# A hybrid decoder layer on one core: buffer places, deferred sums and engine choice in its MLP tail

## Chip, core and metric

One core of a Trainium2 chip runs the whole layer. The engines are TensorE (PE, the matrix products), VectorE (DVE), ScalarE (ACT) and GpSimd (POOL); SyncE (SP) issues most transfers, in order, as ACT does a few. The metric is the device time of one execution in microseconds (us), less is better.

## What is computed

The reference is a decoder layer on 1024 tokens of width 1024 in float32: three branches (a matrix-memory recurrence, a differential attention, a cross-attention into 256 memory tokens), gates that weigh them, an output projection, and an MLP. Only its end matters here:

```python
merged = g_m * (y_m @ w_proj_m[l]) + g_d * (y_d @ w_proj_d[l]) + g_c * (y_c @ w_proj_c[l])
x = x + merged @ w_out[l]

h2 = rms_norm(x, norm_mlp_g[l])
x = x + jnp.square(jax.nn.relu(h2 @ w_up[l])) @ w_down[l]
```

`w_up` is 1024 x 4096, `w_down` 4096 x 1024.

## The kernel before

All values are held with features on partitions and tokens along the free axis, as tiles of 128 x 512 (two halves `hf` of the tokens). A float32 product is made of three matmuls on a high and a low part of each operand (`mm3`, L119); an operand is split by a cast on ACT (high part) and a subtraction on DVE (low part), by `split` or, in a stretch whose order is pinned, `split2`. Every matmul is written by the helper at L93. A scheduler reorders instructions of DVE, ACT, POOL and SP by its own estimates, while PE keeps the written order in the pinned stretches; the rows below are the order that comes out.

**Merge and output projection** (`tail`, L1410 on). For each branch the products `mm<-kt,w` are weighed with gate tiles. Then `wout` is multiplied: for each of 8 feature tiles and 2 halves, `res` loads a tile of the input x into a `gl` tile (`fetch`, L1418), adds the product (L1476), stores it (x1_d, L1477), squares it (`sq`, L1482), sums the squares on POOL (`ssq`, L1483), and scales it into `h2` (L1485), which is stored. The pool `gl` has two places, which gates and x tiles take in turn.

**Up projection** (`wino`). Products of 2 x 2 blocks are made by seven products instead of eight (Strassen in Winograd's form): a block step n is seven products of three matmuls each, 21 matmuls of 128 x 512. A unit u is one of 16 column blocks of `w_up` and takes four steps (kp 0 to 3, the four row blocks of `h2`); its seven sums p0 to p6 stand in seven of the eight PSUM banks. `raw` loads a weight block (256 KB, `wraw`) and makes four of its eight forms on POOL (L1260 to L1263), `wsp` splits it into `wo`, up to three steps ahead. `wino_x` makes the operand `xo` from `h2` (`xr`, with sums `xts`). Unit 0 is done in two runs, because the last part of `h2` comes late: steps 0 and 1 on kp 0 and 1, then unit 1 (steps 2 to 5), then steps 6 and 7. Its first run's sums are copied to seven `pt` tiles (two of them in `gl`, two in `ssq`).

The factor of the norm (`rb`) is made on the way: `rstd` is a generator; `first(bank)` moves it on at four places between products: `px<-ones,ssq` (sums over the squares), then the reciprocal root and the diagonal tiles `dg`, then two products `px<-dg,ones`, copied by ACT into the two halves of `rb` (L1544).

After a unit `combine` makes four results from the seven sums (one copy on ACT, seven sums on DVE: tiles `u2`, `c11`, `u3`, `c21`, shown as `u` and `c`). `use_up` multiplies each with `rb` on DVE, takes relu and square on ACT into `rq`, stores three of them, and after a `yield` makes the four operand sums `xts` of the down projection (`wino_t`, three on DVE and one on POOL, L1243) and stores them to r_d. For unit 0 (`whole`) `combine` works in place on the `pt` tiles. `todo` says after which step each piece runs.

**Down projection** (`down`). The same scheme: steps of 21 matmuls `p<-xd,wo`; `xd` is the operand read back from r_d (three sums in place 0 to 2, four in 3 to 6), split in place. Its tiles lie in memory that the up projection's tiles leave, and so wait for their last readers. There are three places for raw weights (dwr0 to dwr2). `x02` holds the last two of the first operand's seven forms. Below, d0, d1, ... are the down projection's raw weights in order, x0, x1, ... its operands.

Of the kernel before, what the change touches and what calls it, by code (L numbers as in the profile page):

```python
# [10 lines left out]
F32 = mybir.dt.float32  # L11
# [6 lines left out]
P = 128  # L18
# [55 lines left out]
class Layer:  # L74
# [1214 lines left out]
    def wino(self, ws, load, use, first, parts):  # L1289


        V, A = self.V, self.A
        self.pinned = True

        runs = [(0, (0, 1)), (1, (0, 1, 2, 3)), (0, (2, 3))] + [(u, (0, 1, 2, 3)) for u in range(2, len(ws))]
        raw, wsp, W = self.wino_steps([ws[u][:, kp] for u, kps in runs for kp in kps], self.wrp, self.wop, 3)
        X = {}
        raw()
        wsp(0, self.split)
        X[0] = self.wino_x(0, load)  # L1300
        wsp(0, self.split)
        X[1] = self.wino_x(1, load)
        X[2] = self.wino_x(2, load)
        raw()
        wsp(0, self.split)
        tl = lambda n: self.ev.tile([P, 512], F32, tag=n, name=self.name(n))

        def combine(ms, psum):

            m1, m2, m6, m7, m4, m5, m3 = ms  # L1310
            u2, c11, u3, c21 = m1, m2, m7, m4
            if psum:
                u2, c11, u3, c21 = (tl(n) for n in ("u2", "c11", "u3", "c21"))
                A.copy(u2, m1)
            V.tensor_add(c11, u2, m2)
            V.tensor_add(u2, u2, m6)
            V.tensor_add(u3, u2, m7)
            V.tensor_add(c21, u3, m4)
            V.tensor_add(u3, u3, m5)
            V.tensor_add(u2, u2, m5)  # L1320
            V.tensor_add(u2, u2, m3)
            return u2, c11, u3, c21


        todo = {}
        n = -1
        for r, (u, kps) in enumerate(runs):
            bank = lambda j: f"p{(7 * r + j + 4) % 8}"
            ps = [self.pw.tile([P, 512], F32, tag=bank(j), name=self.name(f"p{j}")) for j in range(7)]
            for kp in kps:  # L1330
                n += 1
                if n == 2:
                    X[3] = self.wino_x(3, load)
                w, x = W[n], X[kp]
                for j, (l, q) in enumerate(self.PROD):
                    self.mm3(ps[j], (w[:, l, 0], w[:, l, 1]), (x[:, q, 0], x[:, q, 1]), kp == kps[0], kp == kps[-1])
                    if (r, kp, j) in ((0, 1, 1), (1, 1, 6), (1, 2, 6), (1, 3, 3)):
                        first(bank(7))
                if kp != kps[-1]:
                    wsp(n)  # L1340
                    for f in todo.pop(n, []):
                        next(f)
            if r == 0:
                part = parts()
                for t, m in zip(part, ps):
                    A.copy(t, m)
                wsp(n)
            elif r == 2:
                for t, m in zip(part, ps):
                    V.tensor_add(t, t, m)  # L1350
                wsp(n)


                def whole():
                    c = combine(part, False)
                    yield
                    yield from use(0, c)

                next(late)
                g = whole()  # L1360
                todo.update({n + 1: [late], n + 3: [g], n + 5: [g], n + 8: [g]})
            else:
                cs = combine(ps, True)
                wsp(n)
                g = use(u, cs)
                if r == 1:
                    late = g
                else:
                    for f in todo.pop(n, []):
                        next(f)  # L1370
                    next(g)
                    todo.setdefault(n + 1, []).append(g)
        for g in sum(todo.values(), []):
            next(g)
        self.nwino = len(runs)
        self.pinned = False
# [35 lines left out]
    def tail(self):  # L1412
        tc, nc, a = self.tc, self.nc, self.a
        V, G = nc.vector, nc.gpsimd
# [1 line left out]
        cut = lambda t, i, hf: t[:, i, hf * 512 : (hf + 1) * 512]  # L1416

        def fetch(d, f, hf):  # L1418
            t = self.gl.tile([P, 512], F32, tag="gl", name=self.name("gl"))
            nc.sync.dma_start(t, half(d, f, hf))  # L1420
            return t

        c9 = ExitStack()
        with ExitStack() as c0:
            E = lambda *x, **k: c0.enter_context(tc.tile_pool(*x, **k))
# [3 lines left out]
            rb = one.tile([P, D], F32, name="rb2")  # L1429
# [4 lines left out]
            with ExitStack() as c1:  # L1434
                E = lambda *x, **k: c1.enter_context(tc.tile_pool(*x, **k))
                self.pmm, self.kmm, self.nmm = Banks(E, "pmm2"), 8, 3
                if True:
# [7 lines left out]
                    rawp = E(name="yrp", bufs=2)  # L1445
                    self.rp = E(name="rp2", bufs=2)
                    self.wp = E(name="wp2", bufs=4)
                    hi = [[mtp.tile([P, 512], F32R, name=f"mh{k}_{hf}") for hf in range(2)] for k in range(NK)]
                    mg, lo = {}, {}
                    for bi, b in enumerate((2, 0, 1)):  # L1450
# [41 lines left out]
            with ExitStack() as c1:  # L1492
                E = lambda *x, **k: c1.enter_context(tc.tile_pool(*x, **k))
                one_ = lambda n: E(name=n, bufs=1)
# [17 lines left out]
                def use_up(u, cs):  # L1512

                    b = self.xrp.tile([P, 4, 512], F32, tag="xr", name=self.name("rq"))
                    for i in (1, 3, 2, 0):
                        hf = i % 2
                        self.V.tensor_mul(cs[i], cs[i], rb[:, hf * 512 : (hf + 1) * 512])
                        self.A.activation(cs[i], cs[i], AF.Relu)
                        self.A.activation(b[:, i], cs[i], AF.Square)
                    self.A.dma_start(self.rd[u, :, 0:3], b[:, 1:4])  # L1520
                    yield
                    t = self.wino_t(b, self.V)
                    nc.sync.dma_start(self.rd[u, :, 3:7], t)
                    yield

# [34 lines left out]
    def down(self):  # L1560
# [4 lines left out]
        with ExitStack() as c1:  # L1565
# [11 lines left out]
            x3 = one_("dx3")  # L1577
            a1 = one_("acc1")
            accum(a1, 14, 0)
            x02 = one_("dx02")  # L1580
            a2 = one_("acc2")
            accum(a2, 4, 0)
            wr = [one_("dwr2")]
            a3 = one_("acc3")
            accum(a3, 8, 768)
            x1, x2 = one_("dx1"), one_("dx2")
            wr = Ring([one_("dwr0"), one_("dwr1")] + wr)
            wo = Ring([one_(f"dwo{i}") for i in range(3)])
            x00 = one_("dx00")
            accs = accs[2:] + accs[:2]  # L1590
# [16 lines left out]
            def xdma(q):  # L1607

                X[q] = []
                for pool, i, n in xp[q % 4]:  # L1610
                    t = pool.tile([P, n, 2, 512], F32R, tag=f"x{i}", name=self.name("xd"))
                    nc.sync.dma_start(f32(t[:, :, 1]), self.rd[kp(q), :, i : i + n])
                    X[q].append(t)

            def xsplit(q, parts=(0, 1, 2), split=self.split2):
                for i, t in enumerate(X[q]):
                    if i in parts:
                        split(t[:, :, 0], t[:, :, 1], f32(t[:, :, 1]))
# [22 lines left out]
            xsplit(0, split=self.split)  # L1641
            wsp(0, self.split, False)
            xdma(1)
            wsp(0, self.split)
            xsplit(1, split=self.split)
            xdma(2)
            wsp(0, self.split)
            xsplit(2, split=self.split)
            xdma(3)
            n = -1  # L1650
            seen = set()
# [248 lines left out]
```

## Time and profile before

| | us |
|---|---|
| median of 3 runs | 2200.8 (2197.91 to 2201.39) |
| profiled execution, its own time | 2198.07 |
| its span on the core | 2196.3 |
| merge and output projection, end of the last wout product | 1561 |
| up projection | 1561 to 1880 |
| down projection | 1880 to 2192 |

The mean granted clock of PE is 0.996 of full speed. A row of the view of waits says which engine and line waited for which, with the total, the count and the longest. A row of the view of windows has the stretch, its length, the busy time of PE, of its weight loads, of DVE, ACT and POOL, with the number of instructions, then the granted clock, the DMA engines' busy share and GB/s. A row of the timeline has start, duration, engine, line, operation, output and inputs, and in brackets how long the engine stood idle before it and what ended that. Rows on a tile give the fewest, median and most ns and the first and last start.

### The profile page before, as it was taken

The numbers are of one execution on the slowest core, as the hardware profiler recorded it, in microseconds if no ns is written. First come the engines' busy times: TensorE is split into PE (matmuls) and PEld (weight loads), VectorE is DVE, ScalarE is ACT, GpSimd is POOL, SyncE is SP. The second block draws the span as 40 slices with busy tenths as digits, with TensorE's granted clock in tenths as the row PEclk, the third lists the DMA queues.
The fourth block names the chain that finished last, engine by engine and source line by source line (L and its number), as shares of the span: only waits on it lengthen the run. The fifth ranks groups of instructions, "written<-read, shape, count | busy, mean of one in ns | idle before, by whom it ended". The sixth has DMA issues, their size and how long they took to land.

```text
span 2196.3 us, 30710 instructions
## 1 busy us (share of the span) xinstructions
PE 2154.0 (98%) x11049; PEld 1853.4 (84%) x11049; DVE 1424.0 (65%) x2678; ACT 1002.6 (46%) x1998; POOL 571.6 (26%) x732
## 2 busy tenths in 40 slices
PE   7999999999999999999999999999999999999999
PEld 5878889898899999999887788888787888788887
DVE  6643565575548777777665433554589877867779
ACT  6543354454346666666554221223444444643332
POOL 2100000000111111111121002202757655665553
PEclk9999999999999999999999999999999999999999
DMA  6123122121443343333343643435435444954444
GB/s 245 37 72 116 60 89 70 44 82 49 157 119 92 96 97 86 86 87 80 108 158 121 206 144 125 139 115 190 155 116 199 157 144 153 330 192 157 145 140 168
DMA packets 137358, 281.46 MB, mean 128 GB/s; under 512 B 13137, under 2 KB 29814, under 8 KB 135158
## 3 DMA queue, kind: packets, MB, share of 16 engines
q1 hardware_dynamic: 130870, 259.58, 37.5%
q10 hardware_dynamic: 6336, 19.93, 2.3%
q8 instruction: 87, 1.43, 0.3%
q14 instruction: 65, 0.53, 0.1%
HBM read 182.95 MB, written 71.34 MB: 116 GB/s over the span
## 4 chain that ended last, share of the span: by engine, by line
PE 79%; DMA 7%; DVE 6%; ACT 3%; POOL 2%; issue 2%; SPq 0%; DVEq 0%; ACTq 0%; POOLq 0%
PE mm L93 46%; PE p L93 21%; PE sc L93 6%; PE po L93 3%; PE tp L96 3%; DMA x_d<-gl 1%; DVE acc L69 1%; DVE wo L69 1%; DMA gl<-in_xT 1%; PE pr L96 1%; DMA xr<-h_d 1%; DVE u L69 1%; DMA kraw<-y 1%; POOL wraw L1262 0%; DVE w L114 0%
## 5 line engine op out<-in xcount | busy, mean ns | idle before, releaser
L93 PE MATMUL mm<-w,hT 128*128 128x384 f32 (+3 forms) x2496 | 472.9, 332 | 2.9 <-ACT w L113 2.4
L93 PE MATMUL mm<-hT,w 128*128 128x512 f32 x1680 | 411.8, 396 | 0.0
L93 PEld LDWEIGHTS mm<-w,hT 128*128 128x128 f32 x2496 | 390.2, 190 | 14.5 <-ACT w L113 3.0
L93 PEld LDWEIGHTS mm<-hT,w 128*128 128x128 f32 x1680 | 308.5, 188 | 64.7
L93 PE MATMUL p<-xo,wo 128*128 128x512 f32 x1344 | 309.7, 392 | 3.1 <-DVE u L69 1.6
L93 PE MATMUL p<-xd,wo 128*128 128x512 f32 x1344 | 307.8, 391 | 3.8 <-DVE u L69 1.9
L93 PEld LDWEIGHTS p<-xd,wo 128*128 128x128 f32 x1344 | 252.9, 189 | 58.5 <-DVE u L69 2.6
L93 PEld LDWEIGHTS p<-xo,wo 128*128 128x128 f32 x1344 | 252.2, 189 | 59.3 <-DVE u L69 3.7
L93 PE MATMUL mm<-kt,w 128*128 128x512 f32 x1152 | 264.5, 391 | 4.0 <-ACT kt L113 2.7
L93 PEld LDWEIGHTS mm<-kt,w 128*128 128x128 f32 x1152 | 216.8, 189 | 51.7 <-ACT kt L113 3.8
L113 ACT CAST w<-raw 128x256 fp32r<-128x256 f32 (+3 forms) x272 | 142.2, 545 | 164.7 <-PE mm L93 123.2
L114 DVE TENSOR_TENSOR w<-raw,w 128x256 fp32r<-128x256 f32 (+3 forms) x272 | 162.7, 619 | 80.0 <-ACT w L113 78.6
L106 ACT CAST wo<-wraw 128x896 fp32r<-128x896 f32 x122 | 115.0, 944 | 206.6 <-PE p L93 112.0
L69 DVE TENSOR_TENSOR wo<-wraw,wo 128x896 fp32r<-128x896 f32 x122 | 144.3, 1200 | 57.0 <-ACT wo L106 57.0
L1260 POOL TENSOR_TENSOR wraw<-wraw 128x128 f32<-128x128 f32 x128 | 95.1, 743 | 238.4 <-DMA wraw<-in_wdown 103.5
L1008 ACT ACTIVATE dpe<-sc,dst,drr 128x256 f32<-128x256 f32 (+7 forms) x128 | 106.8, 834 | 97.6 <-DVE dst L1004 95.4
L129 POOL TENSOR_SCALAR hss<-hss 128x4 f32<-128x4 f32 x8 | 3.3, 411 | 416.0 <-ACT mscr L754 273.3
L1000 DVE CUSTOM_DVE_ANT_0 sc<-sc,tmask 128x256 f32<-128x256 f32 (+7 forms) x128 | 97.0, 758 | 13.3 <-PE sc L93 12.6
L1263 POOL TENSOR_TENSOR wraw<-wraw 128x128 f32<-128x128 f32 x128 | 93.9, 733 | 10.0
L93 PE MATMUL sc<-dk,dq 128*128 128x512 f32 (+3 forms) x384 | 92.2, 348 | 0.0
L1262 POOL TENSOR_TENSOR wraw<-wraw 128x128 f32<-128x128 f32 x128 | 91.8, 717 | 0.0
L106 ACT CAST xd<-xd 128x1536 fp32r<-128x1536 f32 (+2 forms) x36 | 54.9, 1528 | 67.7 <-DMA xd<-r_d 67.7
(308 smaller groups left out, 3087.6 us busy)
## 6 DMA issues: line engine op xcount, KB each, us to landing
dk<-dsg SPq DMA_DIRECT2D x64, 256.0 KB, 4.5
wraw<-in_wup SPq DMA_DIRECT2D x64, 256.0 KB, 3.3
r_d<-xts SPq DMA_DIRECT2D x16, 1024.0 KB, 4.1
wraw<-in_wdown SPq DMA_DIRECT2D x64, 256.0 KB, 3.0
xd<-r_d SPq DMA_DIRECT2D x19, 768.0 KB, 7.3
xd<-r_d SPq DMA_DIRECT2D x14, 1024.0 KB, 7.0
raw<-in_wd SPq DMA_DIRECT2D x32, 384.0 KB, 3.2
kraw<-y SPq DMA_DIRECT2D x24, 512.0 KB, 4.5
```

The costliest lines, as they stand in the source:

```text
L69: return self.tc.keep_in_program_order(f(*a, **k))
L93: self.pin(self.nc.tensor.matmul(out, l, r, start=start, stop=stop))
L96: self.pin(self.nc.tensor.transpose(out, x, self.ident))
L106: self.A.copy(hi, src)
L113: nc.scalar.copy(hi, src)
L114: nc.vector.tensor_sub(lo, src, f32(hi))
L129: g.tensor_scalar(r, ss, 1.0 / width, EPS, op0=ALU.mult, op1=ALU.add)
L1000: V.tensor_tensor_reduce(out=sc[:, 0:n], in0=sc[:, 0:n], in1=self.tmask[:, D - n : D], scale=1.0, scalar=-3.0e38, op0=ALU.add, op1=ALU.max ...
L1008: nc.scalar.activation(pe[c][:, 0:n], sc[:, 0:n], AF.Exp, bias=t8[:, 2 + c : 3 + c], scale=rr[:, i, c : c + 1], accum_out=t8[:, 4 + c : 5 ...
L1260: G.tensor_add(r[:, 4], r[:, 0], r[:, 3])
L1262: G.tensor_sub(r[:, 6], r[:, 1], r[:, 0])
L1263: G.tensor_sub(r[:, 7], r[:, 2], r[:, 5])
```

## The change

Seven edits, all in the tail. (1) `fetch` takes its tiles from a ring of two pools with two places each. (2) The calls of `first` move: the first one product later, the second and third three products earlier, the third reaching `px<-dg,ones` of the first half. (3) Unit 0's seven sums are made in three portions after steps n + 6, n + 10 and n + 14, where n = 7, its products with `rb` after n + 18 and its operand sums after n + 20, instead of n + 3, n + 5 and n + 8. (4) In memory, dwr0 and dwr1 take the place of `x02`, and `x02` theirs; dwr0 and dwr1 then lie on other up weights than before. (5) The first `wsp` and `xsplit` of `down` stand in another order. (6) The second and third first-weight splits and that of operand x2 use `split2`. (7) For unit 15 the four products with `rb` go to GpSimd (`M`), and its operand sums are issued by the unpinned `nc.vector`.

```diff
@@ -1334,7 +1334,7 @@
                 w, x = W[n], X[kp]
                 for j, (l, q) in enumerate(self.PROD):
                     self.mm3(ps[j], (w[:, l, 0], w[:, l, 1]), (x[:, q, 0], x[:, q, 1]), kp == kps[0], kp == kps[-1])
-                    if (r, kp, j) in ((0, 1, 1), (1, 1, 6), (1, 2, 6), (1, 3, 3)):
+                    if (r, kp, j) in ((0, 1, 2), (1, 1, 3), (1, 2, 3), (1, 3, 3)):
                         first(bank(7))
                 if kp != kps[-1]:
                     wsp(n)
@@ -1352,13 +1352,16 @@
 
 
                 def whole():
-                    c = combine(part, False)
-                    yield
-                    yield from use(0, c)
+                    m1, m2, m6, m7, m4, m5, m3 = part
+                    for sums in (((m2, m1), (m1, m6), (m7, m1)), ((m4, m7), (m7, m5)), ((m1, m5), (m1, m3))):
+                        for o, i in sums:
+                            V.tensor_add(o, o, i)
+                        yield
+                    yield from use(0, (m1, m2, m7, m4))
 
                 next(late)
                 g = whole()
-                todo.update({n + 1: [late], n + 3: [g], n + 5: [g], n + 8: [g]})
+                todo.update({n + 1: [late], **{n + i: [g] for i in (6, 10, 14, 18, 20)}})
             else:
                 cs = combine(ps, True)
                 wsp(n)
@@ -1416,7 +1419,7 @@
         cut = lambda t, i, hf: t[:, i, hf * 512 : (hf + 1) * 512]
 
         def fetch(d, f, hf):
-            t = self.gl.tile([P, 512], F32, tag="gl", name=self.name("gl"))
+            t = gls.tile([P, 512], F32, tag="gl", name=self.name("gl"))
             nc.sync.dma_start(t, half(d, f, hf))
             return t
 
@@ -1445,6 +1448,7 @@
                     rawp = E(name="yrp", bufs=2)
                     self.rp = E(name="rp2", bufs=2)
                     self.wp = E(name="wp2", bufs=4)
+                    gls = Ring([self.gl, E(name="gl2", bufs=2)])
                     hi = [[mtp.tile([P, 512], F32R, name=f"mh{k}_{hf}") for hf in range(2)] for k in range(NK)]
                     mg, lo = {}, {}
                     for bi, b in enumerate((2, 0, 1)):
@@ -1512,14 +1516,15 @@
                 def use_up(u, cs):
 
                     b = self.xrp.tile([P, 4, 512], F32, tag="xr", name=self.name("rq"))
+                    V_, M = (nc.vector, G) if u == 15 else (self.V, self.V)
                     for i in (1, 3, 2, 0):
                         hf = i % 2
-                        self.V.tensor_mul(cs[i], cs[i], rb[:, hf * 512 : (hf + 1) * 512])
+                        M.tensor_mul(cs[i], cs[i], rb[:, hf * 512 : (hf + 1) * 512])
                         self.A.activation(cs[i], cs[i], AF.Relu)
                         self.A.activation(b[:, i], cs[i], AF.Square)
                     self.A.dma_start(self.rd[u, :, 0:3], b[:, 1:4])
                     yield
-                    t = self.wino_t(b, self.V)
+                    t = self.wino_t(b, V_)
                     nc.sync.dma_start(self.rd[u, :, 3:7], t)
                     yield
 
@@ -1577,14 +1582,14 @@
             x3 = one_("dx3")
             a1 = one_("acc1")
             accum(a1, 14, 0)
-            x02 = one_("dx02")
+            wr = [one_("dwr0"), one_("dwr1")]
             a2 = one_("acc2")
             accum(a2, 4, 0)
-            wr = [one_("dwr2")]
+            wr.append(one_("dwr2"))
             a3 = one_("acc3")
             accum(a3, 8, 768)
             x1, x2 = one_("dx1"), one_("dx2")
-            wr = Ring([one_("dwr0"), one_("dwr1")] + wr)
+            x02, wr = one_("dx02"), Ring(wr)
             wo = Ring([one_(f"dwo{i}") for i in range(3)])
             x00 = one_("dx00")
             accs = accs[2:] + accs[:2]
@@ -1641,11 +1646,12 @@
             xsplit(0, split=self.split)
             wsp(0, self.split, False)
             xdma(1)
-            wsp(0, self.split)
             xsplit(1, split=self.split)
+            wsp(0)
             xdma(2)
-            wsp(0, self.split)
-            xsplit(2, split=self.split)
+            xsplit(2, (0,))
+            wsp(0)
+            xsplit(2, (1, 2))
             xdma(3)
             n = -1
             seen = set()
```

On SP, near the end of the output projection, before (`gl<-in_xT` loads an x tile, `x_d<-gl` stores the sum, `h_d<-h` stores h2; the last tile is gl_15391):

```order
L1420 DMA gl_15321<-in_xT 128x512
L1506 DMA xr_15548<-h_d 128x2x1024
L1477 DMA x_d<-gl_15286 128x512
L1486 DMA h_d<-h_2479_15293 128x512
L1420 DMA gl_15356<-in_xT 128x512
L1477 DMA x_d<-gl_15321 128x512
L1486 DMA h_d<-h_2483_15328 128x512
L1420 DMA gl_15391<-in_xT 128x512
L1477 DMA x_d<-gl_15356 128x512
L1486 DMA h_d<-h_2487_15363 128x512
```

and after, where the last tile is gl_15394:

```order
L1423 DMA gl_15324<-in_xT 128x512
L1481 DMA x_d<-gl_15209 128x512
L1490 DMA h_d<-h_2467_15216 128x512
L1423 DMA gl_15359<-in_xT 128x512
L1481 DMA x_d<-gl_15244 128x512
L1490 DMA h_d<-h_2471_15251 128x512
L1423 DMA gl_15394<-in_xT 128x512
L1510 DMA xr_15552<-h_d 128x2x1024
L1481 DMA x_d<-gl_15289 128x512
L1490 DMA h_d<-h_2479_15296 128x512
L1481 DMA x_d<-gl_15324 128x512
L1490 DMA h_d<-h_2483_15331 128x512
```

The last tile's load stood behind the store of the tile two before it and now stands ahead of that and of the xr load.

On DVE, at the turn from the up to the down projection, before (`c` and `u` are the sums of unit 15, `wo_18277`, `wo_18294` and `wo_18374` the splits of d1, d2 and d3, `xd_18290` and `xd_18292` the two parts of x2, `xd_18307` and `xd_18309` those of x3):

```order
L69 TENSOR_TENSOR c_2841_18117<-u_2840_18116,p_2832_18017 128x512
L114 TENSOR_TENSOR wo_18277<-wraw_18258,wo_18277 128x7x128
L69 TENSOR_TENSOR u_2840_18116<-u_2840_18116,p_2833_18018 128x512
L69 TENSOR_TENSOR u_2842_18118<-u_2840_18116,p_2834_18019 128x512
L114 TENSOR_TENSOR wo_18294<-wraw_18280,wo_18294 128x7x128
L69 TENSOR_TENSOR c_2843_18119<-u_2842_18118,p_2835_18020 128x512
L114 TENSOR_TENSOR xd_18290<-xd_18290 128x3x512
L69 TENSOR_TENSOR u_2842_18118<-u_2842_18118,p_2836_18021 128x512
L69 TENSOR_TENSOR u_2840_18116<-u_2840_18116,p_2836_18021 128x512
L114 TENSOR_TENSOR xd_18292<-xd_18292 128x4x512
L69 TENSOR_TENSOR u_2840_18116<-u_2840_18116,p_2837_18022 128x512
```

after (`wo_18285`, `wo_18300` and `wo_18378` are d1, d2 and d3, `xd_18294` and `xd_18296` x2, `xd_18311` and `xd_18313` x3, `xts` the operand sums of unit 15):

```order
L69 TENSOR_TENSOR u_2842_18122<-u_2842_18122,p_2836_18025 128x512
L69 TENSOR_TENSOR u_2840_18120<-u_2840_18120,p_2836_18025 128x512
L69 TENSOR_TENSOR xd_18294<-xd_18294 128x3x512
L69 TENSOR_TENSOR u_2840_18120<-u_2840_18120,p_2837_18026 128x512
L69 TENSOR_TENSOR wo_18300<-wraw_18288,wo_18300 128x7x128
L69 TENSOR_TENSOR xd_18296<-xd_18296 128x4x512
L1242 TENSOR_TENSOR xts_18146<-rq_18132 128x512
L1244 TENSOR_TENSOR xts_18146<-rq_18132,xts_18146 128x512
L69 TENSOR_TENSOR xd_18311<-xd_18311 128x3x512
L1245 TENSOR_TENSOR xts_18146<-rq_18132,xts_18146 128x512
L69 TENSOR_TENSOR wo_18378<-wraw_18303,wo_18378 128x7x128
L69 TENSOR_TENSOR xd_18313<-xd_18313 128x4x512
```

Before, two weight splits and two operand splits stand between the sums of unit 15, then four products with rb and the splits of x3 and d3 (and the operand sums behind these); now one split of each kind stands between them, no products follow, and the operand sums stand ahead of d3 and of x3's second part.

On POOL at the same turn, before (`wraw_18280` is d2, `wraw_18297` d3, `xts` unit 15's operand sum):

```order
L1263 TENSOR_TENSOR wraw_18280<-wraw_18280 128x128
L1260 TENSOR_TENSOR wraw_18297<-wraw_18297 128x128
L1262 TENSOR_TENSOR wraw_18297<-wraw_18297 128x128
L1261 TENSOR_TENSOR wraw_18297<-wraw_18297 128x128
L1263 TENSOR_TENSOR wraw_18297<-wraw_18297 128x128
L1260 TENSOR_TENSOR wraw_18339<-wraw_18339 128x128
L1262 TENSOR_TENSOR wraw_18339<-wraw_18339 128x128
L1261 TENSOR_TENSOR wraw_18339<-wraw_18339 128x128
L1263 TENSOR_TENSOR wraw_18339<-wraw_18339 128x128
L1243 TENSOR_TENSOR xts_18142<-rq_18128 128x512
```

and after (`wraw_18288` is d2, `wraw_18303` d3):

```order
L1263 TENSOR_TENSOR wraw_18288<-wraw_18288 128x128
L1522 TENSOR_TENSOR c_2841_18121<-c_2841_18121,rb_13027 128x512
L1522 TENSOR_TENSOR c_2843_18123<-c_2843_18123,rb_13027 128x512
L1522 TENSOR_TENSOR u_2842_18122<-u_2842_18122,rb_13027 128x512
L1260 TENSOR_TENSOR wraw_18303<-wraw_18303 128x128
L1262 TENSOR_TENSOR wraw_18303<-wraw_18303 128x128
L1261 TENSOR_TENSOR wraw_18303<-wraw_18303 128x128
L1263 TENSOR_TENSOR wraw_18303<-wraw_18303 128x128
L1522 TENSOR_TENSOR u_2840_18120<-u_2840_18120,rb_13027 128x512
L1243 TENSOR_TENSOR xts_18146<-rq_18132 128x512
```

Three of the four products stand between the weight sums of d2 and d3, the last behind those of d3.

## The prediction

> **What bounds the kernel now.** I read the page first, then what TensorE (PE) waited for from 1190 us on, since no edit touches anything earlier, then stretches around each wait.
>
> ```profile
> PE 2154.0 (98%) x11049; PEld 1853.4 (84%) x11049; DVE 1424.0 (65%) x2678; ACT 1002.6 (46%) x1998; POOL 571.6 (26%) x732
> ```
>
> PE is busy for 98% of the span and the diff removes no matmul, so only PE's idle time and its half-rate time can be won. The waits of PE from 1190 us to the end (total, times, longest):
>
> ```profile
> PE p L93 <- DVE u L69: 3.5, 4, 1.9
> PE mm L93 <- ACT kt L113: 2.7, 2, 2.1
> PE px L93 <- POOL ssq L1483: 1.7, 1, 1.7
> PE p L93 <- DVE c L69: 1.3, 2, 0.7
> PE p L93 <- POOL wraw L1263: 1.3, 1, 1.3
> ...
> PE p L93 <- DVE wo L69: 0.6, 1, 0.6
> PE px L93 <- ACT rb L1544: 0.6, 1, 0.6
> PE px L93 <- DVE gl L1476: 0.5, 1, 0.5
> ```
>
> The same stretch cut where these waits lie (window and length, busy time of each engine, granted PE clock, DMA share, GB/s), and then three narrow windows:
>
> ```profile
> 1190.00:1240.00 50.00, 46.05 (x190) 35.91 (x189) 22.57 (x24) 18.05 (x20) 0.20 (x1) 0.97 0.63 215
> 1560.00:1580.00 20.00, 17.80 (x79) 14.50 (x78) 11.06 (x11) 14.86 (x20) 13.69 (x13) 0.91 0.67 223
> 1640.00:1685.00 45.00, 41.94 (x177) 31.87 (x176) 39.54 (x45) 22.61 (x34) 30.56 (x37) 1.00 0.56 199
> 1685.00:1835.00 150.00, 150.00 (x664) 124.20 (x663) 122.24 (x145) 68.60 (x104) 98.08 (x138) 1.00 0.44 155
> 1880.00:1900.00 20.00, 16.16 (x61) 12.10 (x61) 18.37 (x18) 14.50 (x16) 12.26 (x14) 0.91 0.89 327
> 1900.00:2165.00 265.00, 265.00 (x1169) 219.14 (x1169) 197.77 (x201) 104.50 (x100) 152.47 (x225) 1.00 0.54 179
> ```
>
> ```profile
> 1217.30:1220.70 3.40, 3.40 (x10) 2.62 (x9) 0.90 (x1) 0.00 (x0) 0.00 (x0) 0.50 0.90 298
> 1572.30:1575.70 3.40, 3.40 (x9) 2.63 (x8) 3.40 (x3) 2.27 (x5) 3.32 (x3) 0.50 0.66 198
> 1889.90:1893.30 3.40, 3.40 (x10) 2.69 (x9) 3.40 (x5) 2.08 (x3) 2.80 (x4) 0.52 0.85 281
> ```
>
> So PE idles 2.2 us at 1560 (20.00 - 17.80), 3.1 us at 1640 and 3.8 us at 1880, and never between. Behind the waits at 1560 and 1880 the clock falls to half for 3.4 us, in which PE does half the work: some 1.6 us more each. With the 0.6 us for rb the recoverable sum is 2.2 + 1.6 + 0.6 + 3.1 + 3.8 + 1.6 = 12.9 us. After 1900 PE is full: nothing can be won there, only lost.
>
> [...]
>
> **The change part by part.**
>
> *Four gl places and px one product later.* In the last projection of the merge (wout), the last x tile is loaded late, because it shares two places with the tile before it. PE's px, the load and its landing, ACT and POOL there:
>
> ```profile
> 1567.93 1.02 PE L93 MATMUL px<-ones,ssq 128*128 128x1 f32 x8 [0.53 <-DVE gl L1476]
> 1570.63 1.05 PE L93 MATMUL px<-ones,ssq 128*128 128x1 f32 x8 [1.67 <-POOL ssq L1483]
> ```
>
> ```profile
> L1420 SPq DMA_DIRECT2D gl<-in_xT x2: 332/332/333, 1559.7 to 1563.7; - x2
> ```
>
> ```profile
> 1563.16 0.63 ACT L1482 ACTIVATE sq<-gl 128x512 f32<-128x512 f32 x1
> ...
> 1564.31 1.47 ACT L113 CAST xo<-xr 128x1536 fp32r<-128x1536 f32 x1
> 1567.88 0.63 ACT L1482 ACTIVATE sq<-gl 128x512 f32<-128x512 f32 x1 [2.10 <-DVE gl L1476]
> ```
>
> ```profile
> 1562.51 2.66 POOL L1483 TENSOR_TENSOR ssq<-ssq,sq 128x512 f32<-128x512 f32 x2 [2.68 <-ACT sq L1482]
> 1568.58 1.99 POOL L1483 TENSOR_TENSOR ssq<-ssq,sq 128x512 f32<-128x512 f32 x1 [3.42 <-ACT sq L1482]
> ```
>
> With four places this load no longer waits for the store of the tile two before it; SP issues it ahead of the next xr load and at the latest where the load at 1559.7 stood, 4 us earlier, so x is there by about 1563 and DVE right behind. ACT still has the xo cast ahead of the last square, so the square runs at 1565.8 to 1566.4 and POOL's sum from 1566.4 to 1567.7 or 1568.4 (1.33 or 1.99). The first half of px is reached at about 1567.4, and three more matmuls (0.7) move it to 1568.1: the second half waits 0.3 at most. Of 3.8 (2.2 and 1.6 at half rate) I take 3.5; ends 2.2 (half rate stays) and 3.8. At the merge's start two 256 KB loads now go ahead of others in SP's queue: at the 215 GB/s of that window 2.4 us if the kt casts, for which PE waits 2.7, came that much later. They are issued before the branch's data is needed, so I take 0; ends -2.4 and +0.5.
>
> *px for the first half of rb three products earlier, its partner as well.* ACT's copy of rb then precedes a wo cast: the 0.6 goes; ends 0 and 0.6.
>
> *Unit 0's sums in portions.* Before, seven sums, then four products with rb and the operand sums stand ahead of other units' adds in one lump, and the 3.1 us at 1640 are PE waiting behind it on DVE. They now lie over 15 later steps (3, 2 and 2 sums, products, operand sums). Prices per instruction, DVE from 1685 to 1835:
>
> ```profile
> L69 DVE TENSOR_TENSOR u<-u,p 128x512 f32<-128x512 f32 x40 | 26.8, 685 | 3.3
> ...
> L69 DVE TENSOR_TENSOR c<-c,rb 128x512 f32<-128x512 f32 x16 | 11.3, 749 | 0.0
> ```
>
> A portion is 2.1 or 1.4 us, the products 3.0. DVE has 150.00 - 122.24 = 27.8 us free in 150, 3.5 in a unit of 19. Every portion fits; the unit with the products and operand sums is nearly full, and the splits of the down projection's first operand also move into it. So of 3.1 I take 2.7; ends 0 (the whole lump comes back) and 3.1.
>
> *Places of down's first weights.* d0 and d1 take places that come free two weights earlier. SP's longest wait around there was for such a place:
>
> ```profile
> SPq L1274 <- DVE wo L69: 30.1, 8, 9.3
> ```
>
> In return x02, a 512 KB part of the first operand, waits for the last up weight's split, and the second part of the next operand (x1), the store of unit 14, d2 and later loads stand behind it on SP. The bytes are the same. DVE and PE before:
>
> ```profile
> 1880.74 1.52 PE L93 MATMUL p<-xd,wo 128*128 128x512 f32 x6
> ```
>
> ```profile
> 1881.53 1.34 DVE L114 TENSOR_TENSOR wo<-wraw,wo 128x896 fp32r<-128x896 f32 x1 [1.70 <-ACT wo L113]
> ...
> 1884.19 1.09 DVE L114 TENSOR_TENSOR wo<-wraw,wo 128x896 fp32r<-128x896 f32 x1
> ...
> 1888.66 2.28 DVE L114 TENSOR_TENSOR xd<-xd 128x2048 fp32r<-128x2048 f32 x1
> 1890.86 0.68 DVE L69 TENSOR_TENSOR u<-u,p 128x512 f32<-128x512 f32 x1
> ...
> 1892.93 1.81 DVE L69 TENSOR_TENSOR u<-u,rb 128x512 f32<-128x512 f32 x2
> ...
> 1897.61 2.28 DVE L69 TENSOR_TENSOR xd<-xd 128x2048 fp32r<-128x2048 f32 x1
> ```
>
> These splits wait on late data between the sums of unit 15, whose PSUM banks PE wants next. With d1 early, only one wo split (1.2) and the smaller xd split (about 1.8, by size against the 2.28) stand between seven sums of 0.68: the last ends at about 1881.3 + 4.8 + 3.0 = 1889.1 instead of 1891.5. PE's 3.8 of idle shrinks to about 1, ends 0.7 and 2.7.
>
> *Unit 15's four products on GpSimd.* DVE gives up 3.4 us, but the operand sums of unit 15 now stand on DVE ahead of the split of weight d3 and of x3, which PE needs for its fourth step. PE came there at 1880.74 + 3 x 4.76 (21 matmuls of 0.2267, 265.00 by 1169) + 3.8 + 1.6 = 1900.4; x3's second part, wanted two products (1.4) later, was ready at 1899.9 (1897.61 + 2.28). POOL's prices, an undisturbed weight sum, one beside DVE's xd split, and a 128x512 operand sum:
>
> ```profile
> 1879.52 0.45 POOL L1261 TENSOR_TENSOR wraw<-wraw 128x128 f32<-128x128 f32 x1
> ...
> 1888.77 2.49 POOL L1263 TENSOR_TENSOR wraw<-wraw 128x128 f32<-128x128 f32 x1
> ```
>
> ```profile
> L1243 POOL TENSOR_TENSOR xts<-rq 128x512 f32<-128x512 f32 x16 | 29.0, 1809 | 8.7 <-DMA r_d<-xts 5.0 <-ACT rq L1519 3.7
> ```
>
> POOL does d3's four weight sums before the last product, and these ended in 1891.3. They depend on a load that is no earlier. The product takes 1.3 (as ssq) to 1.8, relu and square on ACT 1.2 (twice 0.6), then DVE does three operand sums (2.3), two xd splits (4.1) and one wo split (1.1), about 7.9 with a wait or two: x3 is ready between 1890.4 + 9.1 = 1899.5 (sums undisturbed) and 1893.1 + 9.1 = 1902.2. Against 1901.8 that is +2.3 to -0.4. So what the places save is mostly waited for again at the fourth step. I take +1.0 for both edits together, one stretch at half rate still there; ends -2.0 (a second stretch) and +5.4 (all of 3.8 + 1.6). Later splits (d4, x) had no wait after 1900 and DVE is 75% busy there: 0.
>
> Sum: 3.5 + 0 + 0.6 + 2.7 + 1.0 = 7.8. The profiled execution took 2198.1 us (span 2196.3 and 1.8 around it), which becomes 2190.3; the median, 2200.8, stands 2.7 above it and becomes 2193.0.
>
> **The rivals.**
> - All of the transition is won, since POOL's last product comes early enough: +5.4 instead of 1.0, 2188.6. For it: the queue order leaves POOL free before d3 lands. Against it: DMA is 89% busy there.
> - POOL's products are held while DVE works. The same 128x128 sum takes 2.49 in the second of those rows, where DVE splits, against 0.45 in the first. Then the last product waits out a wo and an xd split (3.4): the transition gives about -2.0 and the time is 2196.0. [...]
> - The portions' work comes back as waits at the ends of units 4 to 7, and the transition gives -1: 7.8 - 2.7 - 2.0 = 3.1 won, 2197.7, no change that can be told. Against it: 3.5 us of room in each unit.
> - Slower: x02's load holds SP. x1's second part must be split by the time unit 15's products end (1880.7), since DVE takes its split ahead of the sums, 4 us after landing: from a landing at 1877 on each us costs one, and from 1877 + 7.8 + 4.4 = 1889 on the kernel is slower. It would take the last up weight 10 us late; at a landing of 1894, 2209. For it only the busy queue.
>
> **How the numbers follow.** Chances: forecast 0.45, all won 0.17, products held 0.22, portions come back 0.10, SP held 0.06. About 0.2% (4.4 us) is what this kernel's measurement can tell: faster means below 2196.4. That is nearly all of the first two, 0.6 of the third and little of the fourth: 0.76; within 0.2%: 0.18; slower: 0.06. The range reaches from 2188 (all won) to 2199 (portions come back, or the merge's start loses 2.4 as well); what I call likeliest is 2190 to 2196.
>
> **What would show it.** Right: PE's waits for ssq and gl and the half clock at 1572 gone; no waits of p between 1640 and 1685; sums of unit 15 without late splits between them; a new wait of PE for DVE wo or xd some 15 us into the down projection. Wrong: waits of p between 1700 and 1780, a longer kt wait at 1213, no wait at the fourth step (then 2189), or PE idle again later than 1900.

## The result, and the profile after

The changed kernel takes 2195.54 us (median of 22 executions, 2191.75 to 2199.87), the kernel before, measured beside it, 2199.53 (22 executions): ratio 0.9983, 95% interval 0.9976 to 0.9989, or by the ratio 3.7 us less; the two profiled spans, 2196.3 and 2194.5 us, are 1.8 apart. The forecast was 7.8 us less. The measured change lies inside the bound of 0.2% that counts as no change, near its edge; the prediction had given that outcome 0.18 and a faster kernel 0.76. The time itself lies inside its range, 2188 to 2199.

TensorE's waits from 1190 us to the end, in the changed kernel:

```profile
PE mm L93 <- ACT kt L113: 3.6, 2, 3.0
PE p L93 <- DVE xd L69: 1.6, 1, 1.6
PE p L93 <- DVE u L69: 1.6, 3, 0.8
PE p L93 <- DVE wo L69: 1.6, 1, 1.6
PE p L93 <- ACT wo L106: 1.6, 1, 1.6
PE p L93 <- DVE c L69: 1.4, 1, 1.4
PE p L93 <- POOL wraw L1261: 0.8, 1, 0.8
```

The waits of px for ssq, gl and rb are gone. Stretches of the changed kernel (window and length; busy PE, weight loads, DVE, ACT, POOL; clock, DMA share, GB/s):

```profile
1560.00:1580.00 20.00, 20.00 (x98) 16.81 (x97) 12.95 (x14) 13.38 (x18) 17.76 (x19) 1.00 0.56 184
1640.00:1685.00 45.00, 45.00 (x200) 37.24 (x200) 39.71 (x51) 20.24 (x31) 25.72 (x42) 1.00 0.39 138
1685.00:1765.00 80.00, 78.80 (x344) 63.68 (x342) 70.83 (x82) 41.37 (x64) 54.08 (x71) 1.00 0.52 185
...
1870.00:1890.00 20.00, 17.45 (x73) 12.89 (x71) 15.80 (x14) 12.59 (x15) 15.14 (x13) 1.00 0.95 366
1890.00:1905.00 15.00, 10.19 (x28) 6.97 (x27) 10.57 (x9) 10.93 (x12) 10.18 (x15) 0.77 0.70 249
1905.00:2165.00 260.00, 259.94 (x1147) 215.21 (x1147) 193.62 (x197) 99.01 (x93) 143.04 (x215) 1.00 0.52 171
```

1560 and 1640 are full and at full clock, 1.2 us of idle came up at 1720, and the turn from up to down, now at 1870, is longer: 2.6 and 4.8 us idle, and the clock at 0.77.

Where the up projection begins and where the down projection begins says it best; timeline of PE, before and then after:

```profile
1561.12 5.15 PE L93 MATMUL p<-xo,wo 128*128 128x512 f32 x22
...
1880.07 2.20 PE L93 MATMUL p<-xd,wo 128*128 128x512 f32 x9
```

```profile
1561.15 5.15 PE L93 MATMUL p<-xo,wo 128*128 128x512 f32 x22
...
1871.98 1.52 PE L93 MATMUL p<-xd,wo 128*128 128x512 f32 x6
```

The up projection took 318.95 us and takes 310.84: 8.1 won. From the start of down's first matmul to that of its last it was 311.25 and is 317.57: 6.3 lost. 8.1 - 6.3 = 1.8 is the difference of the two spans. (The start of the up projection moved by 0.03 between these two, though over the fourteen profiled executions it lies anywhere from 1558.2 to 1565.8 us; this is part of what spreads the times.)

In the table, "up" is the first of these lengths and "turn" the time from the start of down's first matmul to the start of its 169th, eight steps, 38.1 us at full rate (168 times the 0.2267 us of a matmul in the full stretch behind 1900 of the kernel before); both from the one profiled execution of each kernel.

| kernel | ratio to before (95%) | up | turn |
|---|---|---|---|
| before | 1 | 318.95 | 44.7 |
| changed | 0.9983 (0.9976 to 0.9989) | 310.84 | 51.0 |
| e3 first three edits (x places, px, portions) | 0.9964 (0.9952 to 0.9976) | 310.85 | 44.6 |
| e10 the same again | 0.9971 (0.9959 to 0.9983) | 310.81 | 45.0 |
| e9 portions alone | 0.9988 (0.9977 to 0.9999) | 316.39 | 45.0 |
| e4 memory and order alone | 1.0029 (1.0018 to 1.0040) | 319.85 | 50.6 |
| e2 first three, memory, order | 0.9987 (0.9979 to 0.9996) | 310.90 | 50.4 |
| e1 the change with its last product on DVE | 0.9985 (0.9975 to 0.9995) | 310.85 | 49.5 |
| e6 first three, memory | 0.9963 (0.9950 to 0.9976) | 310.85 | 48.5 |
| e5 first three, order | 0.9966 (0.9952 to 0.9979) | 310.86 | 50.6 |
| e11 the same again | 0.9978 (0.9968 to 0.9987) | 310.83 | 48.0 |
| e7 first three, products on GpSimd | 0.9960 (0.9949 to 0.9972) | 310.85 | 48.4 |
| e12 the same again | 0.9973 (0.9962 to 0.9984) | 310.85 | 48.2 |
| e8 first three, memory, products | 0.9984 (0.9974 to 0.9995) | 310.86 | 52.8 |

e1 to e4, e5 to e8 and e9 to e12 each ran together, beside the kernel before. The profiled executions of e3 and e10 are the fastest of their 5 and 6, that of e8 the slowest of its 12 (2203.19 us, median 2197.87).

### The profile page after: what moved, and what is told of

Read it like the earlier page. It is cut to its first block, busy times and chain, and to the rows that moved or that the text cites. A ratio compares the mean times of both kernels' runs of the same rounds, so it can differ in the third digit from the quotient of the medians.

```text
span 2194.5 us, 30706 instructions
## 1 busy us (share of the span) xinstructions
PE 2150.9 (98%) x11049; PEld 1852.4 (84%) x11049; DVE 1418.6 (65%) x2674; ACT 1002.7 (46%) x1998; POOL 565.5 (26%) x736
## 4 chain that ended last, share of the span: by engine, by line
PE 87%; DVE 5%; DMA 3%; ACT 2%; issue 1%; POOL 1%; SPq 0%; DVEq 0%; ACTq 0%; POOLq 0%
PE mm L93 51%; PE p L93 23%; PE sc L93 6%; PE po L93 3%; PE tp L96 3%; DVE acc L69 1%; DVE u L69 1%; PE pr L96 1%; DMA kraw<-y 1%; DVE wo L69 0%; DMA xd<-r_d 0%; DVE c L69 0%; PE tp L93 0%; DVE w L114 0%; DMA mx<-in_mem 0%
## 5 line engine op out<-in xcount | busy, mean ns | idle before, releaser
L1260 POOL TENSOR_TENSOR wraw<-wraw 128x128 f32<-128x128 f32 x128 | 93.7, 732 | 246.2 <-DMA wraw<-in_wdown 109.5
L1263 POOL TENSOR_TENSOR wraw<-wraw 128x128 f32<-128x128 f32 x128 | 86.6, 676 | 10.0
L1262 POOL TENSOR_TENSOR wraw<-wraw 128x128 f32<-128x128 f32 x128 | 88.9, 694 | 0.0
```

The lines of the kernel that those rows point to most:

```text
L1260: G.tensor_add(r[:, 4], r[:, 0], r[:, 3])
L1262: G.tensor_sub(r[:, 6], r[:, 1], r[:, 0])
L1263: G.tensor_sub(r[:, 7], r[:, 2], r[:, 5])
```

## The experiments

**What loses at the turn of the changed kernel.** Its trace there: ACT (the casts of x02 and of both parts of x1), POOL (d3's weight sums and the last product), DVE (x1's second split, the first sum of unit 15, its last sum u, the operand sums, d3's split) and PE at the fourth step of down.

```profile
1867.46 4.45 ACT L113 CAST xd<-xd 128x1024 fp32r<-128x1024 f32 x3 [3.81 <-DMA xd<-r_d]
```

```profile
1880.65 1.99 POOL L1260 TENSOR_TENSOR wraw<-wraw 128x128 f32<-128x128 f32 x1
...
1884.41 2.39 POOL L1263 TENSOR_TENSOR wraw<-wraw 128x128 f32<-128x128 f32 x1
1886.77 1.28 POOL L1522 TENSOR_TENSOR u<-u,rb 128x512 f32<-128x512 f32 x1
```

```profile
1871.94 2.29 DVE L114 TENSOR_TENSOR xd<-xd 128x2048 fp32r<-128x2048 f32 x1 [0.26 <-ACT xd L113]
1874.15 0.68 DVE L69 TENSOR_TENSOR c<-u,p 128x512 f32<-128x512 f32 x1
...
1882.24 0.67 DVE L69 TENSOR_TENSOR u<-u,p 128x512 f32<-128x512 f32 x1
...
1889.41 0.69 DVE L1242 TENSOR_TENSOR xts<-rq 128x512 f32<-128x512 f32 x1 [2.93 <-ACT rq L1524]
...
1894.50 1.34 DVE L69 TENSOR_TENSOR wo<-wraw,wo 128x896 fp32r<-128x896 f32 x1
```

```profile
1891.64 0.50 PE L93 MATMUL p<-xd,wo 128*128 128x512 f32 x1 [1.56 <-ACT wo L106]
1893.77 0.51 PE L93 MATMUL p<-xd,wo 128*128 128x512 f32 x1 [1.64 <-DVE xd L69]
1895.89 7.38 PE L93 MATMUL p<-xd,wo 128*128 128x512 f32 x17 [1.61 <-DVE wo L69]
```

u is ready at 1882.9, its product starts at 1886.8 behind d3's sums, the operand sums wait for it 2.9 us on DVE, and what is queued behind holds PE for 4.8 us in three waits of one step: d3's cast on ACT, behind the relu of u, then x3's and d3's splits on DVE, behind the operand sums. That gave theory 1: GpSimd's queue loses it. The first kernel takes only the last product back:

```diff
-                        M.tensor_mul(cs[i], cs[i], rb[:, hf * 512 : (hf + 1) * 512])
+                        (self.V if i == 0 else M).tensor_mul(cs[i], cs[i], rb[:, hf * 512 : (hf + 1) * 512])
```

> The changed kernel, but the last of unit 15's four products (u2) goes back to VectorE; the other three stay on GpSimd. Theory 1 (the u2 product stands behind d3's four sums on GpSimd, 1880.7 to 1886.8 in the trace of the changed kernel, though u2 is ready at 1882.9, and the operand sums, d3's and x3's splits wait for it): the product ends near 1884.8, some 3.2 us earlier, TensorE's 4.8 us at the fourth step of down shrink to about 1.5 and the two half-rate windows behind it to none or one: 3 to 6 us faster than the changed kernel, 2190 to 2193. Theory 2 (down's early steps wait for loads and for d3 itself, whatever makes the product): the same stall, within 1 us of the changed kernel.

The time is that of the changed kernel (0.9985 beside 0.9983). DVE in e1:

```profile
1885.63 2.54 DVE L69 TENSOR_TENSOR xd<-xd 128x2048 fp32r<-128x2048 f32 x1
1888.23 0.81 DVE L1242 TENSOR_TENSOR xts<-rq 128x512 f32<-128x512 f32 x1
...
1893.44 1.34 DVE L69 TENSOR_TENSOR wo<-wraw,wo 128x896 fp32r<-128x896 f32 x1
```

Down's first matmul starts at 1872.95 in this trace, 1.0 us later than in that of the changed kernel, so times are compared from there. The product is made on DVE and ends 3.3 us earlier, as expected, but x2's split now stands between it and the operand sums, which start 2.2 us earlier (15.3 against 17.4), not 3.2, and d3 follows them. Theory 1 explains 1.5 us of the turn (51.0 to 49.5), not 6.

All four products back on DVE, the rest of the change kept:

```diff
-                    V_, M = (nc.vector, G) if u == 15 else (self.V, self.V)
...
-                        M.tensor_mul(cs[i], cs[i], rb[:, hf * 512 : (hf + 1) * 512])
+                        self.V.tensor_mul(cs[i], cs[i], rb[:, hf * 512 : (hf + 1) * 512])
...
-                    t = self.wino_t(b, V_)
+                    t = self.wino_t(b, self.V)
```

> The changed kernel with all four products of unit 15 back on VectorE; places and the rest of the change stay. Theory 1: GpSimd's queue is out of the chain, but 3.1 us of products now stand on VectorE ahead of x2's second split, so TensorE waits about 2.6 us at the third step and again 2.5 for x3's second part: about as long as the changed kernel, 2194 to 2197, with the waits in other places. Theory 2: the same time and the same place of the wait, the fourth step.

Time and turn stay (0.9987, 50.4), the places of the waits change: 3.0 for u at the end of the first step, 1.2 for x3 at the fourth, 1.7 for an accumulation at the fifth. The time is as theory 1 had it, and the place did not stay, as it would have by theory 2; but of the two places that theory 1 named only x3 came (1.2 instead of 2.5), the third step did not wait. GpSimd is not needed for the loss.

None of the turn's edits (three edits on the kernel before):

> The kernel before with the four x places, the moved px calls and unit 0's sums in portions; the turn from up to down as before (no exchange of places, no GpSimd products). By the trace of the changed kernel these edits make the down projection start 8.1 us earlier (1872.0 against 1880.1) and theory 1 says that the turn gives 4 to 6 back: this kernel should be 7 to 8 us faster than before, about 2192. If theory 1 is wrong and the profiled turn of the changed kernel was an accident of that execution, this kernel is no faster than the changed one, 2195.

As expected, 0.9964. Its waits from 1865 to 1905 are those of before at 1880:

```profile
PE p L93 <- DVE u L69: 1.9, 1, 1.9
PE p L93 <- POOL wraw L1263: 1.2, 1, 1.2
PE p L93 <- DVE c L69: 0.6, 1, 0.6
```

So the loss is that of the edits at the turn. Exchange of places and order of splits on the kernel before:

> The kernel before with only the exchange of places and the order of down's first splits. The forecast's step: the sums of unit 15 end earlier and up to 2.8 of TensorE's 3.8 us at the turn go, then VectorE's four products delay x2's second split: a net of +1 to -2 us, 2197 to 2201. Theory 2 (the splits on late data were not what held the sums): no change in the waits at 1881 to 1889 and 2199.5.

Slower, by 0.0029 (6.4 us), where +1 to -2 was expected: the two edits that should free the sums cost as much as the whole loss, and the interval of e2, which has these two beside the first three, lies wholly above that of e3.

**Which of them.** The exchange is two things, memory and the order (with `split2`) of down's first splits; with the products (and the unpinned operand sums that go with them) these make three edits, each added alone to e3. The first two:

```diff
-            x02 = one_("dx02")
+            wr = [one_("dwr0"), one_("dwr1")]
...
-            wr = [one_("dwr2")]
+            wr.append(one_("dwr2"))
...
-            wr = Ring([one_("dwr0"), one_("dwr1")] + wr)
+            x02, wr = one_("dx02"), Ring(wr)
```

```diff
-            wsp(0, self.split)
             xsplit(1, split=self.split)
+            wsp(0)
...
-            wsp(0, self.split)
-            xsplit(2, split=self.split)
+            xsplit(2, (0,))
+            wsp(0)
+            xsplit(2, (1, 2))
```

> The first three edits (x places, px calls, portions) and only the new order and form of down's first splits; memory and unit 15's products as before. Here VectorE's queue has x2's second split, x3's first part and one operand sum of unit 15 ahead of d3's split, and two more ahead of x3's second part. Theory A (this order loses the time): the turn is as long as in the kernels with all of the exchange, first to last down matmul 316 to 318 us instead of 311.7, and the time 2195 to 2197. Theory B (the memory exchange loses it, since the load of x02 holds SP): 311 to 313 us and 2190 to 2191.

> The first three edits and only the memory exchange (d0 and d1 two weights earlier, x02 later); order and form of the splits as before, so d3 and x3 are split ahead of unit 15's operand sums. Theory A: d1's split no longer waits, 1.2 us of TensorE's first wait goes, the rest of the turn stays: 310 to 312 us from first to last down matmul, 2189 to 2191. Theory B: 316 to 318 us and 2195 to 2197.

> The first three edits and only unit 15's products on GpSimd. Here the order on VectorE keeps x3 and d3 ahead of the operand sums, and the 3.1 us of products are gone from it. Theory A: TensorE's waits for the sums of unit 15 (3.8 us) stay, as they come before the products, and nothing waits at the fourth step: 311 to 312 us, 2190 to 2191, no gain by the products alone. Theory C (the products on GpSimd are themselves what loses): 315 to 318 us, 2194 to 2197.

> The first three edits, the memory exchange and the products on GpSimd, with the splits in the order of before: the whole change without its new order of down's first splits. Theory A: d3 stands ahead of the operand sums, x3's second part behind them: 310 to 313 us, 2189 to 2192, some 4 us faster than the changed kernel. Theory B or C: 315 to 318 us and 2194 to 2197.

Neither theory A nor B holds alone: in the traces the turn is longer with each of the three edits (48.0 to 50.6 us beside 44.6 and 45.0), each time by another wait.

Memory (e6): ACT's casts of x02 and x1 in e6 and the first sum of unit 15 on DVE, then that sum in e3:

```profile
1866.44 4.26 ACT L113 CAST xd<-xd 128x1024 fp32r<-128x1024 f32 x3 [4.92 <-DMA xd<-r_d]
```

```profile
1872.94 0.68 DVE L69 TENSOR_TENSOR c<-u,p 128x512 f32<-128x512 f32 x1
```

```profile
1869.44 0.67 DVE L69 TENSOR_TENSOR c<-u,p 128x512 f32<-128x512 f32 x1
```

ACT stands idle 4.9 us for the late x02, x1 is split behind it, and the sums of unit 15 stand behind x1 on DVE: they start 3.1 us after down's first matmul (1869.85), in e3 0.9 before it (1870.33). With d1 early the wait put down to POOL falls from 1.2 to 0.8, and the late x02 costs more: PE's waits from 1865 to 1905 are 5.3 us, against 3.7 in e3. That is no more than the 5.3 of e9, whose turn is 45.0; the rest of e6's 48.5 goes with 10.2 us at half rate, against none in the turn of e9 and 3.4 in that of e3.

Order (e5), waits of PE from 1865 to 1905:

```profile
PE p L93 <- DVE u L69: 3.0, 1, 3.0
PE p L93 <- DVE xd L69: 2.8, 1, 2.8
PE p L93 <- POOL wraw L1261: 1.4, 1, 1.4
PE p L93 <- DVE wo L69: 1.0, 1, 1.0
```

The wait for u grows from 1.9 to 3.0, and 3.8 us for d3 and x3, behind the operand sums, is new. In e11, the same kernel, they are 2.5 for u, 1.8 for x3, none for d3, and 1.0 for an accumulation.

Products (e7): the relu of the first product on ACT, d2's cast, and d2's split on DVE:

```profile
1875.70 0.63 ACT L1523 ACTIVATE c<-c 128x512 f32<-128x512 f32 x1 [2.81 <-POOL c L1522]
1876.24 0.92 ACT L113 CAST wo<-wraw 128x896 fp32r<-128x896 f32 x1
```

```profile
1877.25 1.09 DVE L114 TENSOR_TENSOR wo<-wraw,wo 128x896 fp32r<-128x896 f32 x1 [1.74 <-ACT wo L113]
```

ACT waits for GpSimd with the cast of d2 queued behind, and between the sums of unit 15 DVE waits for that cast. PE waits 2.5 for c and 3.2 for u instead of 0.6 and 1.9, in e12 the same.

Memory and products together (e8) lose as much as the whole change, 0.9984, without the new order; their median is 4.3 to 5.6 us above those of e5 to e7 beside them. So neither the order nor the products are needed for the loss. Whether the memory is, stays open: every kernel that lost by time has it, and order and products without it were not run. By time the single edits were not told from none: e5, e6 and e7 had the ratio of e3 within their intervals of 0.0013 either way, though e3 did not run beside them. So the order and the products were repeated beside the first three alone (e10), and the portions alone added:

> The kernel before with only unit 0's sums in portions. From the first up matmul to the first down matmul took 318.95 us before and 310.85 with the first three edits. The forecast's terms for them are 3.5 (x places and px), 0.6 (px) and 2.7 (portions), and 8.1 was measured for all three: this kernel should show 318.95 - 2.7 = 316.2 if the portions gave what was forecast, and 314.9 if the whole excess of 1.3 is theirs; in time 2.7 to 4 us less than before.

> The first three edits once more, beside the next two. By the traces its turn (168 matmuls, eight steps, from the first down matmul) takes 44.6 us, that of the kernel with the new order 50.6 and that with GpSimd's products 48.4. If the traces stand for the executions, this kernel is 3 to 6 us faster than those two in one call; if the single profiled executions were unlucky, all three have the same time.

> The first three edits and the new order of down's first splits, again, with memory and products as before. If the traces stand for the executions: turn 50.6 us and 4 to 6 us slower than the first three alone. If not: the same as those within 1.5 us, and a turn that differs from 50.6 in this second trace.

> The first three edits and unit 15's products on GpSimd, again, in the old order of splits. If the traces stand for the executions: turn 48.4 us and 3 to 4 us slower than the first three alone, since ACT's relu of the first product waits for GpSimd ahead of d2's cast. If not: the same as the first three within 1.5 us.

e9 took 316.39 us for up, 2.6 less than before, as forecast. Side by side the medians are 2192.4 (e10), 2195.3 (order) and 2194.0 (products): the signs agree with the traces, the sizes are 2.9 and 1.6 us (by the ratios 1.5 and 0.4) where the traces say 3.0 to 6.0 and 3.2 to 3.8, and the intervals of the ratios overlap. The 4 to 6 and 3 to 4 us that were expected did not come. That the order alone and the products alone lose is shown by two traces each, not by the times; for the memory alone there is one trace, and most of what it lost there is half rate. Shown by both is that memory and order together lose (e4, e2 against e3). In the traces the three edits do not add: 3.0 to 6.0, 3.5 to 3.9 and 3.2 to 3.8 alone, 6.0 to 6.4 together. That each puts its wait where another's would have been is my reading of the waits, not shown apart.

## Why the prediction was right in part

- *x places and px:* forecast 3.5. The matmul 105 places behind up's first starts 30.64 us after it before, 26.55 after: 4.1. Right in kind; the listed idle time counts from a matmul's modelled end, and what a stop costs from start to start is more (1.56 listed for the first at the fourth step of down, 1.71 from start to start). px now runs as one:

```profile
1567.95 1.84 PE L93 MATMUL px<-ones,ssq 128*128 128x1 f32 x16
```

- *Merge start:* forecast 0, up starts 0.03 later. The longer wait for kt, named as a sign of being wrong, did come (3.6 us, 2.7 before), but it is 5.3 in e1 and 1.3 in e3 with the same edit, and 3.1 in e4 without it: it goes with the execution, not with the edit.
- *rb:* forecast 0.6, measured 1.2 (126 places behind the first: 37.49 to 32.22, less the 4.1).
- *Portions:* forecast 2.7, measured 2.6 alone (e9), 2.8 in the changed kernel. What came back, 1.2 us, is in the unit that was named, with the operand sums of unit 0 and the first splits of down:

```profile
1721.43 1.76 PE L93 MATMUL p<-xo,wo 128*128 128x512 f32 x6 [0.77 <-DVE u L69]
```

- *Places and products:* forecast +1.0, ends -2.0 and +5.4; measured -6.3 in the trace, outside both ends. This is the term that failed. It took the loads of down's start as unchanged in time because their bytes were, and let only the fourth step lose. In place of that, ACT stood 3.8 us for the late x02, with x1's casts behind it; x1's split ended 2.3 us after unit 15's last product on PE (1874.2 against 1872.0) and held the first sum, the mechanism that I had priced only as the slower rival (0.06). So unit 15's last sum ended 10.9 us after down's first matmul, against 11.5 before, where 2.4 us sooner was forecast, and of PE's 3.8 us of waits for these sums 2.6 stayed, not about 1. Then d3's sums took 6.1 us on GpSimd (1880.65 to 1886.8), not 1.9 to 4.6: 1.99, 0.47, 1.32 and 2.39 us each, the first and the last beside the two parts of x2's split on DVE (2.24 us from 1880.07, 2.37 from 1884.12); and x3's and d3's splits stood on DVE behind the operand sums that waited for it. My start of down was also read from a row that the window had cut: 1880.74 stood for 1880.07, which put the fourth step 0.7 us too late.
- *The new wait at the fourth step* was forecast, at up to 0.4 us net; it is 4.8 us and a half-rate stretch of twice the length (1895.62 to 1902.45 at a clock of 0.50, before 1889.73 to 1893.14; by estimate half of PE's 6.56 busy us in it, 3.3, lost instead of the forecast's 1.6). That it replaces what the places save was right, its size was not.

That the time came out inside the range is luck as far as the turn goes: an error of +1.3 before it stands against one of -7.3 at it, and the range, wide enough for 1.8 us won, took in the rest. The 2193.0 was counted from a median before of 2200.8; from 2199.53 the same 7.8 would have given 2191.7. The executions show part of the error at the turn: beside e3 and e10 (0.9964, 0.9971) the whole change gives back 2.6 to 4.2 us. Nearest to the measured 2195.54 is the rival of the held products, 2196.0: d3's sums were slow beside DVE's splits, but the 3.4 us for which it has the last product wait out two splits do not show: that product took 1.28 us (1886.77), in e7 the last two took 2.52 together. (By its own figures, 17 us lost and 7.8 won, the slower rival's 2209 would be 2210.)

## What to carry to other kernels

A queue order is part of the change: before crediting a split that "no longer waits", list what now stands ahead of it on its own engine and on the engine that makes its other half, with the time each becomes ready. Freeing a place for one load by giving another load a later one is an exchange on the in-order queue; price the late one by the first instruction behind it, not by bytes. Edits that repair single waits deep inside a busy stage (the first three) did what their rows said, while those at a turn where all queues are full each moved the wait; here no kernel was told to be faster than the first three edits alone (0.9964 and 0.9971).

## What the runs showed of the hardware

The clock's fall is not set by the length of a stop alone. The same kernel, profiled twice (e5, then e11; a stop and the stretch behind it):

```profile
1874.80:1878.30 3.50, 0.46 (x3) 0.04 (x1) 3.04 (x4) 2.22 (x2) 2.92 (x4) 1.00 1.05 402
1878.30:1881.80 3.50, 3.50 (x15) 2.89 (x16) 3.50 (x5) 2.24 (x3) 2.15 (x3) 1.00 0.64 205
```

```profile
1878.80:1881.70 2.90, 0.39 (x3) 0.00 (x1) 2.90 (x4) 1.90 (x1) 1.36 (x4) 1.00 1.06 404
1881.70:1885.10 3.40, 3.40 (x8) 2.75 (x9) 3.40 (x6) 1.68 (x2) 1.26 (x1) 0.51 0.86 281
```

After 3.0 us of idle PE ran on at full clock (1.00), after 2.5 it ran 3.4 us at half (0.51). What differs, in my reading, is how the stop lies to steps of 3.413 us. In the traces of the kernel before and of the changed kernel the granted clock stands at 0.50 for 3.413 us or twice that, and the stretches start whole multiples of 3.413 us apart: from merge to turn, in the kernel before at 1217.30, 1572.29 and 1889.73 (104 and 93 times 3.413), in the changed kernel at 1216.37 and 1895.62 (199 times). Cut by such steps, counted from the half-rate stretches of its own trace, e5's stop lies across two windows, 44% and 45% idle, and e11's in one that is 74% idle:

```profile
1873.31:1876.73 3.42, 1.92 (x8) 0.97 (x6) 2.27 (x3) 3.42 (x3) 1.43 (x1) 1.00 1.06 410
1876.73:1880.14 3.41, 1.88 (x8) 1.57 (x9) 3.41 (x6) 0.86 (x2) 2.72 (x4) 1.00 0.73 281
```

```profile
1878.33:1881.74 3.41, 0.90 (x5) 0.42 (x4) 3.05 (x4) 2.23 (x2) 1.40 (x4) 1.00 1.04 396
```

The turns of the kernel before and of the changed kernel, cut in the same way:

```profile
1886.31:1889.73 3.42, 1.52 (x7) 0.95 (x6) 3.42 (x4) 2.78 (x2) 2.95 (x4) 1.00 1.05 402
1889.73:1893.14 3.41, 3.41 (x10) 2.64 (x9) 3.41 (x5) 2.09 (x3) 2.81 (x3) 0.50 0.85 281
```

```profile
1888.80:1892.21 3.41, 1.78 (x7) 0.93 (x5) 2.76 (x3) 3.41 (x4) 2.75 (x3) 1.00 0.55 231
1892.21:1895.62 3.41, 0.51 (x1) 0.19 (x1) 3.41 (x3) 1.17 (x1) 3.33 (x3) 1.00 0.08 36
1895.62:1902.45 6.83, 6.56 (x15) 4.75 (x16) 3.68 (x3) 5.87 (x8) 2.52 (x6) 0.50 1.00 336
```

Half rate followed a window that was 56% idle before and one that was 85% idle in the changed kernel; behind one that was 48% idle there the clock stayed at 1.00. A share of idle time at which the clock falls is not shown: in the merge of the kernel before, the half rate at 1572.29 followed a window, 1568.87 to 1572.29, that was 49% idle (PE busy 1.75 of 3.42 us, with products of px in it). So this stop cost itself alone in e5, and in e11 itself and, by estimate, half of the 3.4 us behind it, some 1.7, and one profiled execution is not the mean: e5 and e11 differ by 2.6 us in the turn.
